# Seven block products instead of eight in the up products of both feed-forward parts of a decoder step

## Chip, cores and metric

The kernel runs on one core of one Trainium2 chip, as one program. The metric is its time on the device in microseconds (us), lower is better.

## What is computed

One inference step of a one-layer decoder on 1024 prompt tokens and 64 sample tokens (1088 columns in all), model width 1024, feed-forward width 2816, in float32. A half feed-forward, a mix of windowed attention and linear attention, and a second half feed-forward follow each other:

```python
def _rmsnorm(x, gain):
    y = xf * lax.rsqrt(jnp.mean(xf * xf, axis=-1, keepdims=True) + EPS)
    return (y * gain.astype(jnp.float32)).astype(x.dtype)

def _half_ffn(x, gain, w1, w3, w2):
    h = _rmsnorm(x, gain)
    return x + 0.5 * ((jax.nn.silu(h @ w1) * (h @ w3)) @ w2)
...
yp = _half_ffn(yp, ffn1_norm, ffn1_w1, ffn1_w3, ffn1_w2)
m, kp, vp, sp = _mix_prompt(_rmsnorm(yp, mix_norm), w_in, ..., w_out)
yp = yp + m
yp = _half_ffn(yp, ffn2_norm, ffn2_w1, ffn2_w3, ffn2_w2)
```

The same three steps run for the sample tokens, whose attention also reads a cache of 2048 rows; the cache windows, shifted by 8 rows, are outputs too.

## The kernel before, in words

Activations stand transposed: `xT` is 128 partitions (a feature within its tile of 128) by 8 tiles by 1088 tokens. Every product of the projections is made of two-part operands. A float32 matrix is split into a high part of type fp32r (by a cast, ScalarE in `split`, L128) and a low part (input minus high part, GpSimd or VectorE, L132), and three matmuls per contraction tile of 128 give high x high, high x low and low x high (`project`, L304 for all products with `hH` and `hL`).

Stages on TensorE, in order: first feed-forward part (0 to about 800 us), projections with linear attention and the sample's attention beside them, prompt attention (to about 1500), output projection (`out_proj`), second feed-forward part (from about 1600 to the end).

A feed-forward part (`ffn`) goes over 22 blocks of 128 features, and for each over three chunks of tokens (`CH`: 364, 362, 362 columns, one PSUM bank each). `project` makes the *up products* h w1 and h w3 of a block (24 matmuls each, PSUM tile `ps1`, shown as `ps`). `gate` multiplies both by 1/rms (`rstd`), applies silu, multiplies them and splits the result into `g`. `h` is x times the gain in two parts, `hH` and `hL`, made tile by tile and chunk by chunk by `norm_part` (L152, L153), which also adds up the squares; `norm_finish` sums these over partitions by a product with ones (L190) and `rsqrt_wide` turns them into 1/rms. After every group of two or three blocks (`GROUPS`) the *down products* (`two`, L255, PSUM tile `ps2`, shown as `ps`) go over 8 output tiles and the three chunks and add into `xT` (L260); w2's blocks `raw2` are split into `hl2` by VectorE alone, in three buffers.

`_Weights` holds the up weights of one block (1 MB, `raw`), loaded two blocks ahead on SP's queue and split one block ahead into `hl` by ScalarE and GpSimd, two instructions of 1024 columns each. `self.copies` are DMA copies of the cache windows in 32 pieces, one issued per block. `out_proj` goes over the eight output tiles and for each over the three chunks (PSUM tile `pso`), and adds into `xT` (L1096); its weights and those of the second part are one sequence in one pool.

Within a pool, the order in which the program is written and a scheduler that works ahead of the run set each engine's instruction order; every engine then works strictly in that order. PSUM has eight banks that rotate (`_Bank`).

## Time and profile before

| | us |
|---|---|
| three runs | 2395.7, 2398.52, 2396.24 |
| median of runs | 2396.24 |
| span of the profiled execution | 2393.6 |
| TensorE busy (matmul) | 2340.4 |
| VectorE busy | 1193.9 |
| ScalarE busy | 675.2 |
| GpSimd busy | 519.4 |

Matmuls are pipelined, so their durations overlap: the time per matmul is read from the distance of their starts, or from a window divided by its count, not from the mean duration. An x behind a group is the number of its instructions, and "idle before" is what its engine waited just ahead of it, with what ended the wait.

### The profile page before, as it was taken

The page shows a single profiled execution, that of the slowest core. Times are in us where ns is not written, and L with a number is a line of the kernel's source. Part 1 is how long each engine was busy: PE and PEld are TensorE (multiplying, and loading weights), DVE is VectorE, ACT ScalarE, POOL GpSimd, SP SyncE. Part 2 cuts the span into 40 slices and gives each one's busy share as a digit, 9 for nine tenths or more (in the row PEclk, how much of TensorE's full clock was granted, in tenths as well). Part 3 has the DMA queues.
Part 4 walks back from the last instruction along what each step waited for, and adds up shares of the span by engine and source line. Part 5 has one row for each costly group of instructions (what it writes and reads, how often), then busy time and mean ns, then how long its engine had stood idle before and what let it go on. Part 6 is the DMA issues. An engine that isn't in the chain of part 4 may idle for free.

```text
span 2393.6 us, 36628 instructions
## 1 busy us (share of the span) xinstructions
PE 2340.4 (98%) x15089; PEld 2201.1 (92%) x15089; DVE 1193.9 (50%) x2434; ACT 675.2 (28%) x1432; POOL 519.4 (22%) x413
## 2 busy tenths in 40 slices
PE   7999999999999998999997999999999999999999
PEld 7999999999999987888775666999999999999999
DVE  8552434344343769655536887445344342434333
ACT  5111020101101523445446777334111101020110
POOL 5011020201100327301104444343101101020100
PEclk9999999999999999999998999999999999999999
DMA  6345542524250341688965432414244333111002
GB/s 196 125 162 189 195 152 97 211 97 154 84 192 28 111 148 55 189 293 310 360 212 152 123 105 86 174 36 162 92 156 157 113 134 141 44 54 45 28 17 85
DMA packets 126023, 327.15 MB, mean 137 GB/s; under 512 B 21040, under 2 KB 96032, under 8 KB 118176
## 3 DMA queue, kind: packets, MB, share of 16 engines
q1 hardware_dynamic: 107232, 313.41, 38.3%
q10 hardware_dynamic: 16512, 5.11, 0.9%
q0 software_dynamic: 2112, 6.29, 0.7%
q8 instruction: 118, 1.93, 0.3%
q14 instruction: 49, 0.40, 0.1%
HBM read 299.49 MB, written 132.64 MB: 181 GB/s over the span
## 4 chain that ended last, share of the span: by engine, by line
PE 89%; DVE 6%; DMA 2%; issue 1%; ACT 1%; POOL 1%; SPq 0%; DVEq 0%; POOLq 0%; ACTq 0%
PE ps L304 43%; PE ps L255 21%; PE psg L304 10%; PE pso L304 4%; PE psO L1030 2%; PE psS L970 2%; PE psT L1009 2%; PE psA L848 1%; PE psW L889 1%; DVE hL L153 1%; PE psD L668 1%; DVE gs L539 1%; PE pss L457 1%; DVE rstd L168 1%; DVE hl L132 1%
## 5 line engine op out<-in xcount | busy, mean ns | idle before, releaser
L304 PE MATMUL ps<-hH,hl 128*128 128x362 f32 (+1 forms) x4224 | 1044.8, 328 | 7.6 <-ACT hl L128 6.8
L304 PEld LDWEIGHTS ps<-hH,hl 128*128 128x128 f32 x4224 | 747.3, 188 | 11.6 <-ACT hl L128 6.8
L304 PE MATMUL ps<-hL,hl 128*128 128x362 f32 (+1 forms) x2112 | 691.9, 328 | 2.2 <-DVE hL L153 1.9
L255 PE MATMUL ps<-g,hl 128*128 128x362 f32 (+1 forms) x3168 | 529.2, 328 | 0.0
L255 PEld LDWEIGHTS ps<-g,hl 128*128 128x128 f32 x3168 | 526.9, 188 | 0.0
L132 POOL TENSOR_TENSOR hl<-raw,hl 128x1024 fp32r<-128x1024 f32 (+1 forms) x98 | 242.8, 2500 | 1212.1 <-ACT hl L128 1211.6
L304 PEld LDWEIGHTS ps<-hL,hl 128*128 128x128 f32 x2112 | 398.0, 188 | 4.2 <-DVE hL L153 2.8
L304 PE MATMUL psg<-hH,hl 128*128 128x384 f32 (+3 forms) x1200 | 311.2, 331 | 0.0
L260 DVE SCALAR_TENSOR_TENSOR xT<-ps,xT 128x362 f32<-128x362 f32 (+1 forms) x384 | 204.3, 534 | 196.9 <-PE ps L255 188.4
L215 ACT ACTIVATE t<-t 128x364 f32<-128x364 f32 x132 | 66.8, 507 | 785.1 <-DVE t L214 784.9
L216 DVE TENSOR_TENSOR t<-ps,rstd 128x364 f32<-128x364 f32 x132 | 70.6, 535 | 417.5 <-PE ps L304 417.5
L304 PEld LDWEIGHTS psg<-hH,hl 128*128 128x128 f32 (+1 forms) x1200 | 209.3, 184 | 10.0 <-issue 5.9
L304 PE MATMUL psg<-hL,hl 128*128 128x384 f32 (+3 forms) x600 | 197.6, 329 | 0.2 <-DVE hL L153 0.2
L128 ACT CAST hl<-raw 128x1024 fp32r<-128x1024 f32 (+2 forms) x148 | 124.3, 885 | 172.4 <-PE ps L304 111.1
L128 ACT CAST g<-t 128x364 fp32r<-128x364 f32 x132 | 65.1, 494 | 346.5 <-DVE t L217 346.4
L132 DVE TENSOR_TENSOR g<-t,g 128x364 fp32r<-128x364 f32 x132 | 107.1, 813 | 93.2 <-ACT g L128 92.8
L214 DVE TENSOR_TENSOR t<-ps,rstd 128x364 f32<-128x364 f32 x132 | 70.5, 535 | 154.4 <-PE ps L304 153.1
L304 PEld LDWEIGHTS psg<-hL,hl 128*128 128x128 f32 (+1 forms) x600 | 110.6, 184 | 6.4 <-issue 3.8
L132 DVE TENSOR_TENSOR hl<-raw,hl 128x384 fp32r<-128x384 f32 (+3 forms) x178 | 107.1, 610 | 7.7 <-ACT hl L128 3.4
L304 PE MATMUL pso<-hH,hl 128*128 128x362 f32 (+1 forms) x384 | 93.7, 325 | 0.2 <-DVE o L1040 0.2
L217 DVE TENSOR_TENSOR t<-t,t 128x364 f32<-128x364 f32 x132 | 74.5, 565 | 17.8 <-ACT t L215 4.1
L990 ACT ACTIVATE e<-e,s 128x128 f32<-128x128 f32 (+3 forms) x96 | 75.4, 786 | 17.3 <-DVE s L977 17.1
(211 smaller groups left out, 2235.8 us busy)
## 6 DMA issues: line engine op xcount, KB each, us to landing
out_wk<-in_ck SPq DMA_DIRECT2D x16, 3060.0 KB
out_wv_s<-in_cv SPq DMA_DIRECT2D x16, 3060.0 KB
kt<-in_kin SPq DMA_DIRECT2D x24, 1280.0 KB
vt<-in_vin SPq DMA_DIRECT2D x60, 512.0 KB
raw<-in_w13b SPq DMA_DIRECT2D x22, 1024.0 KB
raw<-in_w13a SPq DMA_DIRECT2D x21, 1024.0 KB
raw<-in_w2a SPq DMA_DIRECT2D x48, 192.0 KB
raw<-in_w2b SPq DMA_DIRECT2D x48, 192.0 KB
```

The source lines that it names most:

```text
L128: nc.scalar.copy(hi, x)
L132: e.tensor_tensor(out=lo, in0=x, in1=hi.bitcast(F32), op=ALU.subtract)
L214: nc.vector.tensor_tensor(out=t1[:, :n], in0=p1[:, :n], in1=r, op=ALU.mult)
L215: nc.scalar.activation(t1[:, :n], t1[:, :n], AF.Silu)
L216: nc.vector.tensor_tensor(out=t3[:, :n], in0=p3[:, :n], in1=r, op=ALU.mult)
L217: nc.vector.tensor_tensor(out=t3[:, :n], in0=t3[:, :n], in1=t1[:, :n], op=ALU.mult)
L255: self.mm(p[:, :n], lhsT=hl[:, wt, j, :], rhs=g[:, gp, :n], start=i == 0, stop=i == 3 * nf - 1)
L260: nc.vector.scalar_tensor_tensor(out=xs, in0=p[:, :n], scalar=0.5, in1=xs, op0=ALU.mult, op1=ALU.add)
L304: self.mm(p[:m, :n], lhsT=hl[:, wt, k, cs], rhs=h[:, k, h0 : h0 + n], start=i == 0, stop=i == 23)
L970: self.mm(p[:, :mm], lhsT=q[:, 128 * n : 128 * n + 128], rhs=kk[:, o : o + mm], start=x == 0, stop=x == 1,)
L990: nc.scalar.activation(e[:, :w], e[:, :w], AF.Exp, scale=-1.0, bias=s[:, j : j + 1], accum_out=s[:, 2:3])
L1009: nc.tensor.transpose(p[:, j], es[n][:, 128 * k : 128 * k + 128], self.ident)
```

## The change

The up products become block products. A *unit* is now the four blocks A11, A12, A21, A22 of one weight matrix (w1 or w3) for a pair of feature blocks: 128 output features by 512 contraction features each, as one tile of 128 x 4 x 512. The tokens are processed in two halves of 544, and a half's activations are four blocks of 512 features by 272 tokens. `_Factors.prep` makes the seven left operands of a unit (`ORDER`: A11, S1, S2, A12, S3, A22, S4), where the S are sums and differences of the blocks made on GpSimd, and splits each into `op`, of which there are six buffers. `fill` makes the seven right operands for a half of the tokens (`hH[:, 0..6]`, `hL[:, 0..6]`) from x, times gain, times 1/rms, with differences in between. `product` multiplies one left by one right operand (12 matmuls of 272 columns) into one of three PSUM banks X, Y, Z of the unit, some of them on top of one another; `keep` copies a bank out to SBUF and `result` adds such copies to a later state of a bank to get the four outputs of the unit, then applies silu (w1) or multiplies and splits (w3). 1/rms is no longer applied in the gate.

With it: the units are loaded and prepared once for each half; down products go over two chunks of 272 tokens per half, in groups of up to four blocks; `hl2` has two buffers of four blocks and its high part is cast by ScalarE; the output projection goes over four chunks of 272, its last two output tiles half by half; squares are added up by `squares`; the copies of the cache windows are 64 pieces instead of 32; the second part's weight pool is opened behind the output projection. `w13` is laid out for the units on the host.

```diff
-CH = ((0, 364), (364, 362), (726, 362))
+HALF = 544
+Q = 272
+CQ = tuple((Q * c, Q) for c in range(4))
-GROUPS = ((0, 2), (2, 2), (4, 3), (7, 3), (10, 3), (13, 3), (16, 3), (19, 3))
+GROUPS = ((0, 2), (2, 4), (6, 4), (10, 4), (14, 4), (18, 4))
+OPS = 6
...
+class _Factors:
...
+    ORDER = ("A11", "S1", "S2", "A12", "S3", "A22", "S4")
...
+    def prep(self):
+        u, i = divmod(self.made, 7)
+        if u >= len(self.units) // 2 * (self.half + 1):
+            return
+        self.made += 1
+        nc, raw = self.k.nc, self.raw[u]
+        a11, a12, a21, a22 = (raw[:, q] for q in range(4))
+        def add(out, x, y, op):
+            nc.gpsimd.tensor_tensor(out=out, in0=x, in1=y, op=op)
+        if i == 0:
+            src = a11
+        elif i == 1:
+            src = self.pool.tile([P, 512], F32, tag="s1", name="s1", bufs=1)
+            self.s1[u] = src
+            add(src, a21, a22, ALU.add)
+        elif i == 2:
+            add(a21, a11, a21, ALU.subtract)
+            add(a11, self.s1.pop(u), a11, ALU.subtract)
+            src = a11
+        elif i == 3:
+            src = a12
+        elif i == 4:
+            src = a21
+        elif i == 5:
+            src = a22
+        else:
+            add(a12, a12, a11, ALU.subtract)
+            src = a12
+        op = self.pool.tile([P, 2, HALF], F32R, tag="op", name="op", bufs=OPS)[:, :, :512]
+        self.k.split(src, op[:, 0], op[:, 1], el="pool" if i in (3, 5) else "dve")
+        self.op[u, i] = op
+        if i == 6:
+            del self.raw[u]
+            self.load(u + 2)
...
+    def fill(self, pool, H, gain):
         nc = self.nc
+        b = {}
+        def start(j, kh, n):
+            t = pool.tile([P, 4, Q], F32, tag="op", name="fb", bufs=OPS)
+            s = slice(HALF * H + Q * n, HALF * H + Q * n + Q)
+            for k in range(4):
+                nc.scalar.activation(t[:, k], self.xT[:, 4 * kh + k, s], AF.Copy, scale=gain[:, 4 * kh + k : 4 * kh + k + 1])
+            nc.vector.tensor_tensor(
+                out=t, in0=t, in1=self.rstd[:, s].unsqueeze(1).broadcast_to([P, 4, Q]), op=ALU.mult
+            )
+            b[j] = t
+        def put(i, t):
+            hi, lo = self.block(i)
+            nc.scalar.copy(hi, t)
+            nc.vector.tensor_tensor(out=lo, in0=t, in1=hi.bitcast(F32), op=ALU.subtract)
+        def sub(x, y, out):
+            nc.vector.tensor_tensor(out=out, in0=x, in1=y, op=ALU.subtract)
+        start(11, 0, 0)
+        put(0, b[11])
+        start(12, 0, 1)
+        sub(b[12], b[11], b[11])
+        put(1, b[11])
+        start(22, 1, 1)
+        sub(b[22], b[11], b[11])
+        put(2, b[11])
+        start(21, 1, 0)
+        put(3, b[21])
+        sub(b[22], b[12], b[12])
+        put(4, b[12])
+        sub(b[21], b[11], b[21])
+        put(5, b[21])
+        put(6, b[22])
...
+        def product(U, i):
+            n = "XZXYXXZ"[i]
+            first = (U, n) not in banks
+            p = bank(U, n, first)
+            op = w.op.pop((U, i))
+            hi, lo = self.block(i)
+            m = 0
+            for k in range(4):
+                for wt, h in ((0, hi), (0, lo), (1, hi)):
+                    self.mm(
+                        p,
+                        lhsT=op[:, wt, 128 * k : 128 * k + 128],
+                        rhs=h[:, k],
+                        start=first and m == 0,
+                        stop=m == 11,
+                        skip_group_check=True,
+                    )
+                    m += 1
+            w.prep()
+            return p
...
+        def result(U, j, n, p, other=None):
+            u = U % 22
+            f, m = 2 * (u // 2) + j, u % 2
+            if m == 0:
+                t = pool.tile([P, Q], F32, tag="s", name="s", bufs=5)
+                silu[f, n] = t
+                if other is not None:
+                    nc.vector.tensor_tensor(out=t, in0=p, in1=other, op=ALU.add)
+                    p = t
+                nc.scalar.activation(t, p, AF.Silu)
+                return
+            t = pool.tile([P, Q], F32, tag="t", name="t", bufs=4)
+            s = silu.pop((f, n))
+            if other is not None:
+                nc.vector.tensor_tensor(out=t, in0=p, in1=other, op=ALU.add)
+                nc.gpsimd.tensor_tensor(out=t, in0=t, in1=s, op=ALU.mult)
+            else:
+                nc.vector.tensor_tensor(out=t, in0=p, in1=s, op=ALU.mult)
+            if f not in gts:
+                gts[f] = pool.tile([P, 2, HALF], F32R, tag="g", name="g", bufs=5)
+            c = slice(Q * n, Q * n + Q)
+            self.split(t, gts[f][:, 0, c], gts[f][:, 1, c], el="dve")
...
+        def head(U):
+            keep(U, "a", product(U, 0))
+        def body(U):
+            product(U, 1)
+            keep(U, "b", product(U, 2))
+            result(U, 0, 0, product(U, 3), out.pop((U, "a")))
+            keep(U, "c", product(U, 4))
+            result(U, 1, 1, banks[U, "Z"], out.pop((U, "c")))
+        def tail(U):
+            result(U, 1, 0, product(U, 5))
+            result(U, 0, 1, product(U, 6), out.pop((U, "b")))
+            for n in "XYZ":
+                del banks[U, n]
...
-            hl = pool.tile([P, 2, 3, 128], F32R, tag="hl2", name="hl2", bufs=3)
-            self.split(raw[:, :nf], hl[:, 0, :nf], hl[:, 1, :nf], eh="dve", el="dve")
+            hl = pool.tile([P, 2, 4, 128], F32R, tag="hl2", name="hl2", bufs=2)
+            self.split(raw[:, :nf], hl[:, 0, :nf], hl[:, 1, :nf], eh="act", el="dve")
...
+        for H in range(2):
+            late = None
+            head(22 * H)
+            for u in range(22):
+                U = 22 * H + u
+                body(U)
+                if late is not None:
+                    two(H, late)
+                    late = None
+                gi = ends.get(u // 2 * 2 + 1) if u % 2 else None
+                if gi is not None:
+                    for d in range(2):
+                        load2(gi, d)
+                if u < 21:
+                    head(U + 1)
+                tail(U)
+                if gi is not None:
+                    prep2(gi, 0)
+                    late = gi
+                if self.copies and U > 1:
+                    self.tc.keep_in_program_order(self.copies.pop(0)())
+                next(beside, None)
+            if H == 0:
+                self.fill(w.pool, 1, gain)
+                w.half = 1
+                for _ in range(OPS - 1):
+                    w.prep()
             else:
+                before_last()
+            two(H, late)
...
+        order = [(d, c) for d in range(6) for c in range(4)]
+        order += [(d, 2 * H + n) for H in range(2) for d in (6, 7) for n in range(2)]
...
+                        w.load(0, 4)
+                        w.load(1)
+                        for k in (0, 4):
+                            load_x(1, k, 4)
+                        for k in range(8):
+                            for c in range(2):
+                                self.squares(fp, k, c, first=True)
+                        self.norm_finish(fp, ps, (0, 1), False)
+                        w.prep()
+                        self.fill(wp, 0, self.g1)
+                        for _ in range(OPS - 2):
+                            w.prep()
...
+                        self.out_proj(ps, w, row_done)
+                        self.norm_finish(fp, ps, (2, 3), False)
+                    with pool("wts") as wp, pool("ffn") as fp, pool("ps", space=PSUM) as ps0:
+                        ps = _Bank(ps0, 8)
+                        w = _Factors(self, wp, up("w13b"))
+                        w.load(0)
+                        w.load(1)
+                        w.prep()
+                        self.fill(wp, 0, self.g2)
+                        for _ in range(OPS - 2):
+                            w.prep()
...
-        w = np.stack([g[n + "_w1"].reshape(1024, NF, 128), g[n + "_w3"].reshape(1024, NF, 128)], 2)
-        out["w13" + s] = c(w.reshape(8, 128, NF, 256).transpose(2, 1, 0, 3))
+        w = np.stack([g[n + "_w1"], g[n + "_w3"]]).reshape(2, 2, 4, 128, NF // 2, 2, 128)
+        out["w13" + s] = c(w.transpose(4, 0, 3, 5, 1, 2, 6)).reshape(NF, 128, 4, 512)
```

**Places in the order.** A row is a line, an operation, and out<-in by the program's names with a buffer number; x is a repeat.

First place: GpSimd in a stretch of the first part, between two groups of down products. `raw` are a block's or unit's weights, `hl` and `op` the split operands, `s1` the sum S1, `t` a gate's result. Before:

```order
L132 TENSOR_TENSOR hl_964<-raw_552,hl_964 128x1024 x2
L132 TENSOR_TENSOR hl_1162<-raw_969,hl_1162 128x1024 x2
L132 TENSOR_TENSOR hl_1584<-raw_1167,hl_1584 128x1024 x2
L132 TENSOR_TENSOR hl_1778<-raw_1589,hl_1778 128x1024 x2
L132 TENSOR_TENSOR hl_1977<-raw_1783,hl_1977 128x1024 x2
```

Now, somewhat more than one unit's work (L152 additions, L194 low halves, L359 the gate's product):

```order
L152 TENSOR_TENSOR s1_2112<-raw_1936 128x512
L194 TENSOR_TENSOR op_2012<-raw_1783,op_2012 128x512
L152 TENSOR_TENSOR raw_1936<-raw_1936 128x512
L152 TENSOR_TENSOR raw_1783<-raw_1783 128x512
L194 TENSOR_TENSOR op_2046<-raw_1783,op_2046 128x512
L152 TENSOR_TENSOR raw_1936<-s1_2112,raw_1936 128x512
L359 TENSOR_TENSOR t_2117<-t_2117,s_1974 128x272
L152 TENSOR_TENSOR s1_2273<-raw_2079 128x512
L194 TENSOR_TENSOR op_2165<-raw_1936,op_2165 128x512
L152 TENSOR_TENSOR raw_2079<-raw_2079 128x512
```

Where one split of a block stood behind another, additions, low halves and gate products of several units now alternate.

Second place: ScalarE in the same part (L190 is the high half's cast, L339 the copy of a PSUM bank X in `keep`):

```order
L190 CAST hl2_1357<-raw2_1296 128x512
L190 CAST op_931<-raw_609 128x512
L190 CAST hl2_1446<-raw2_1298 128x512
L339 COPY b_934<-psX_833 128x272
L190 CAST op_951<-s1_949 128x512
L190 CAST op_974<-raw_609 128x512
L190 CAST g_957<-t_954 128x272
L190 CAST op_998<-raw_609 128x512
L339 COPY c_977<-psX_833 128x272
L339 COPY a_1001<-psX_985 128x272
L190 CAST op_1015<-raw_609 128x512
L190 CAST op_1034<-raw_609 128x512
```

The casts of `op` stand between copies of `psX`; several operands of a unit are cast ahead of the next copy of that bank, and w2's casts stand among them.

Third place: VectorE at the start of the first part. `hL` is the low half of the activations, `nsq` a square, `nv` and `nt` are steps of 1/rms, `fb` the scaled blocks in `fill`, `qg` and `kg` gains that `constants` loads, `raw2` the first block of w2. Before, in its first rows:

```order
L153 SCALAR_TENSOR_TENSOR hL_78<-xT_85,g1_64,hH_77 128x364
L168 TENSOR_TENSOR rstd_61<-rstd_61,nsq_112 128x364
L153 SCALAR_TENSOR_TENSOR hL_78<-xT_85,g1_64,hH_77 128x364 x2
L168 TENSOR_TENSOR rstd_61<-rstd_61,nsq_120 128x364
L153 SCALAR_TENSOR_TENSOR hL_78<-xT_85,g1_64,hH_77 128x364
L168 TENSOR_TENSOR rstd_61<-rstd_61,nsq_125 128x364
```

Now:

```order
L241 TENSOR_SCALAR nv_162<-psn_160 128x272
L245 SCALAR_TENSOR_TENSOR nt_153<-nt_153,nv_152 128x272
L246 SCALAR_TENSOR_TENSOR rstd_61<-nt_153,rstd_61 128x272
L274 TENSOR_TENSOR fb_173<-fb_173,rstd_61 128x1088
L274 TENSOR_TENSOR fb_199<-fb_199,rstd_61 128x1088
L245 SCALAR_TENSOR_TENSOR nt_163<-nt_163,nv_162 128x272
L1393 TENSOR_SCALAR qg_386<-qg_386 128x1
L1395 TENSOR_SCALAR kg_389<-kg_389 128x1
L282 TENSOR_TENSOR hL_78<-fb_173,hH_77 128x1088
L246 SCALAR_TENSOR_TENSOR rstd_61<-nt_163,rstd_61 128x272
L1404 CAST e2r_402<-e2_400 128x128
L194 TENSOR_TENSOR hl2_577<-raw2_516,hl2_577 128x256
```

The first low half of activations (L282) now stands behind 1/rms, behind the scaling of two blocks and behind `qg` and `kg`; the low half of w2's first block stands ahead of the rest of the fill.

## Rows read from the trace of the kernel before

**Rows 1.** The page: busy time by engine, then the chain that ended last.

```profile
PE 2340.4 (98%) x15089; PEld 2201.1 (92%) x15089; DVE 1193.9 (50%) x2434; ACT 675.2 (28%) x1432; POOL 519.4 (22%) x413
...
PE 89%; DVE 6%; DMA 2%; issue 1%; ACT 1%; POOL 1%; SPq 0%; DVEq 0%; POOLq 0%; ACTq 0%
PE ps L304 43%; PE ps L255 21%; PE psg L304 10%; PE pso L304 4%; PE psO L1030 2%; PE psS L970 2%; PE psT L1009 2%; PE psA L848 1%; PE psW L889 1%; DVE hL L153 1%; PE psD L668 1%; DVE gs L539 1%; PE pss L457 1%; DVE rstd L168 1%; DVE hl L132 1%
```

**Rows 2.** Windows: us, busy us (x instructions) per engine, clock, DMA share, GB/s.

```profile
0.00:25.00 25.00, 12.29 (x39) 10.87 (x40) 19.29 (x24) 14.54 (x29) 16.53 (x19) 0.87 0.80 266
0.00:50.00 50.00, 35.12 (x160) 32.15 (x161) 43.90 (x65) 25.95 (x49) 27.98 (x27) 0.90 0.60 191
300.00:600.00 300.00, 300.00 (x1813) 299.18 (x1813) 115.27 (x210) 43.18 (x70) 45.47 (x18) 1.00 0.39 142
1560.00:2393.00 833.00, 829.96 (x5041) 828.96 (x5039) 340.04 (x623) 140.46 (x234) 133.52 (x64) 1.00 0.26 91
```

**Rows 3.** Instructions by line: matmuls of up and down products.

```profile
L304 PE MATMUL ps<-hH,hl 128*128 128x362 f32 (+1 forms) x4224 | 1044.8, 328 | 7.6 <-ACT hl L128 6.8 <-POOL hl L132 0.8
L304 PE MATMUL ps<-hL,hl 128*128 128x362 f32 (+1 forms) x2112 | 691.9, 328 | 2.2 <-DVE hL L153 1.9 <-DVE kg L1235 0.3
...
L255 PE MATMUL ps<-g,hl 128*128 128x362 f32 (+1 forms) x3168 | 529.2, 328 | 0.0
```

**Rows 4.** Timeline of TensorE, two places: start us, us, engine, line, operation.

```profile
889.18 0.41 PE L553 MATMUL psL<-gh,bor 128*128 128x270 f32 x2
889.43 0.34 PE L304 MATMUL psg<-hL,hl 128*128 128x384 f32 x1
889.61 0.41 PE L553 MATMUL psL<-gh,bor 128*128 128x270 f32 x2
...
1405.42 0.98 PE L1009 MATMUL psT<-ident,e 128*128 128x128 f32 x7
1406.16 0.48 PE L970 MATMUL psS<-kh,q 128*128 128x512 f32 x1
```

**Rows 5.** Instructions by line and shape: xcount, busy us, mean ns, idle before.

```profile
L132 DVE TENSOR_TENSOR hl<-raw,hl 128x512 fp32r<-128x512 f32 x48 | 36.0, 778 | 1.0 <-ACT hl L128 0.6 <-DMA vt<-in_vin 0.2
...
L128 ACT CAST hl<-raw 128x512 fp32r<-128x512 f32 x52 | 29.8, 615 | 44.8 <-PE psg L304 44.8
...
L1012 ACT COPY pt<-psT 128x384 f32<-128x384 f32 x36 | 17.8, 495 | 1.7 <-PE psT L1009 1.5
...
L152 ACT ACTIVATE hH<-xT,g 128x362 fp32r<-128x362 f32 x32 | 17.0, 585 | 1.1 <-DMA xT<-in_xT 0.8 <-PE pso L304 0.4
...
L166 ACT ACTIVATE nsq<-xT 128x362 f32<-128x362 f32 x32 | 15.9, 497 | 6.3 <-POOL rstd L168 6.3
...
L645 DVE TENSOR_TENSOR vx<-psR,cmask 128x1024 f32<-128x1024 f32 x9 | 11.0, 1220 | 0.5 <-ACT kd L640 0.5
```

**Rows 6.** Timeline at 416 us, VectorE, then GpSimd.

```profile
416.19 0.54 DVE L217 TENSOR_TENSOR t<-t,t 128x362 f32<-128x362 f32 x1
418.03 1.50 DVE L132 TENSOR_TENSOR g<-t,g 128x362 fp32r<-128x362 f32 x1 [1.30 <-ACT g L128]
419.55 0.54 DVE L214 TENSOR_TENSOR t<-ps,rstd 128x364 f32<-128x364 f32 x1
...
416.73 5.05 POOL L132 TENSOR_TENSOR hl<-raw,hl 128x1024 fp32r<-128x1024 f32 x2 [54.82 <-ACT hl L128]
```

**Rows 7.** Timeline of the start: GpSimd, then VectorE.

```profile
4.75 0.79 POOL L164 TENSOR_TENSOR nsq<-xT 128x364 f32<-128x364 f32 x1 [3.75 <-DMA xT<-in_xT]
...
13.81 3.11 POOL L132 TENSOR_TENSOR hl<-raw,hl 128x512 fp32r<-128x512 f32 x2
16.88 5.24 POOL L164 TENSOR_TENSOR nsq<-xT 128x362 f32<-128x362 f32 x5
...
17.24 1.12 DVE L153 SCALAR_TENSOR_TENSOR hL<-xT,g,hH 128x364 fp32r<-128x364 f32 x1
18.28 1.12 DVE L168 TENSOR_TENSOR rstd<-rstd,nsq 128x364 f32<-128x364 f32 x1
```

More of the change, by code (lines that the diff above doesn't have):

```diff
@@ L116, in ahead, with __init__, load @@
         self.load(j + 2)
+class _Factors:
+    ORDER = ("A11", "S1", "S2", "A12", "S3", "A22", "S4")
+    def __init__(self, k, pool, units):
+        self.k, self.pool, self.units = k, pool, units
+        self.raw, self.s1, self.op = {}, {}, {}
+        self.made, self.half = 0, 0
+    def load(self, u, parts=2):
+        if u >= len(self.units):
+            return
+        self.raw[u] = self.pool.tile([P, 4, 512], F32, tag="raw", name="raw", bufs=2)
+        n = 4 // parts
+        for q in range(0, 4, n):
+            self.k.nc.sync.dma_start(out=self.raw[u][:, q : q + n], in_=self.units[u][:, q : q + n])
+    def prep(self):
[32 more added lines that the diff above has]
+            self.load(u + 2)
 class _Kernel:
@@ L143, in rsqrt, with squares, scaled @@
         nc.vector.tensor_tensor(out=y, in0=y, in1=t, op=ALU.mult)
-    def norm_part(self, pool, k, c, gain, first=False):
+    def squares(self, pool, k, c, first=False):
         nc = self.nc
-        c0, n = CH[c]
+        c0, n = CQ[c]
         s = slice(c0, c0 + n)
+        x = self.xT[:, k, s]
+        if k == 0:
+            nc.scalar.activation(self.acc[:, s], x, AF.Square)
+            return
+        sq = pool.tile([P, Q], F32, tag="t", name="nsq", bufs=4)
+        if first and k in (2, 5, 7):
+            nc.gpsimd.tensor_tensor(out=sq, in0=x, in1=x, op=ALU.mult)
+        else:
+            nc.scalar.activation(sq, x, AF.Square)
+        e = nc.vector if first else nc.gpsimd
+        e.tensor_tensor(out=self.acc[:, s], in0=self.acc[:, s], in1=sq, op=ALU.add)
+    def scaled(self, k, s, gain):
+        nc = self.nc
         x = self.xT[:, k, s]
@@ new lines, in ffn, with bank, keep @@
+    def ffn(self, pool, ps, w, gain, w2, before_last, after, beside=iter(())):
+        nc = self.nc
+        gts, w2t, raw2 = {}, {}, {}
+        ends = {f0 + nf - 1: gi for gi, (f0, nf) in enumerate(GROUPS)}
+        banks, out, silu = {}, {}, {}
+        def bank(U, n, start):
+            if (U, n) not in banks:
+                banks[U, n] = ps.tile([P, 512], F32, tag="b", name="ps" + n)[:, :Q]
+            return banks[U, n]
+        def product(U, i):
[18 more added lines that the diff above has]
+            return p
+        def keep(U, name, p):
+            t = pool.tile([P, Q], F32, tag="abc", name=name, bufs=6)
+            nc.scalar.copy(t, p)
+            out[U, name] = t
+        def result(U, j, n, p, other=None):
[8 more added lines that the diff above has]
+                nc.scalar.activation(t, p, AF.Silu)
+                return
+            t = pool.tile([P, Q], F32, tag="t", name="t", bufs=4)
[3 more added lines that the diff above has]
+                nc.gpsimd.tensor_tensor(out=t, in0=t, in1=s, op=ALU.mult)
+            else:
+                nc.vector.tensor_tensor(out=t, in0=p, in1=s, op=ALU.mult)
[16 more added lines that the diff above has]
+                del banks[U, n]
@@ L346, in columns @@
             return chunks(j, width, use)
[L348 removed]
+        yield from columns(0, P, G["q"], scale=32.0**-0.5, first=lambda: self.norm_finish(pool, ps, range(4), tag="t1", bufs=2))
         yield from columns(1, P, G["k"])
```

212 lines of the change are left out of this document (70 added, 142 removed).

## The prediction

> **What bounds the kernel now.** I read the busy table and the chain first. TensorE is busy 98% of the span, VectorE 50%, ScalarE 28%, GpSimd 22%, and the chain that ended last lies on TensorE for 89%: 43% in the up products (L304 into ps), 21% in the down products (L255), 4% in the output projection (pso) [rows 1]. Busy time of pipelined matmuls says little about their rate, so I went to the windows and divided time by matmuls. In 300 to 600 us TensorE runs 1813 matmuls in 300 us, 165.5 ns each for 362 or 364 columns; from 1560 us to the end, output projection, hand-over and second part together, it is the same rate, 5041 in 833 [rows 2]. There a matmul saved is time saved, and the hand-over costs nothing today. Only the start is loose: 160 matmuls in the first 50 us, 26.5 us of work, so 23.5 us are lost [rows 2].
>
> The up products are 4224 + 2112 = 6336 matmuls, the down products 3168 [rows 3], the output projection 8 tiles x 3 chunks x 24 = 576: 10,080 in all, 1668 us at 165.5 ns.
>
> **Matmuls, the gain.** Seven products of 12 matmuls per unit, 22 units, two halves, two parts: 7392 up matmuls of 272 columns. Down products go from three chunks of tokens to four: 4224; output projection likewise: 768. Together 12,384. Their spacing: two of 270 columns take 0.25 us (889.18 to 889.43), so 125 ns; 384 columns (889.43 to 889.61) about 180 ns [rows 4]. I take 125 for 272 (123.5 to 127). Seven of 128 columns take 0.74 us, 106 ns [rows 4]: weight loads alone would allow that, so they don't set 125. 12,384 x 0.125 = 1548 us: **-120 us** (-96 to -139). Up products alone give -125, the other two +5.
>
> The Trainium skill ("TensorE: Matmul & The Clock Gate", Back-to-back issue gap) speaks against the change here: in a stream of weight load and matmul pairs it gives about 81 ns per matmul at 128 columns and 131 at 512. By a line through these, an estimate, 10,080 matmuls at 112 ns are 1125 us and 12,384 at 100 ns are 1235: a loss of 110 us. The trace does not agree (165.5 ns at 362, 106 at 128), and the sum goes by the trace.
>
> **Operand preparation, the cost that was covered.** Before, a weight block is split in two GpSimd instructions per feature block and nothing more. Now each unit needs four GpSimd additions of 512 columns and two GpSimd splits, five VectorE splits, seven ScalarE casts, three PSUM copies, and per pair of units three GpSimd multiplications and four VectorE splits of 272. All that has to be made at TensorE's pace, 12 x 0.125 = 1.50 us per product.
>
> ScalarE: 7 x 0.615 + 3 x about 0.4 (0.495 for 384) [rows 5], plus four silu or casts of about 0.4, is 7.1 us of a unit's 10.5. It is covered. GpSimd and VectorE are not independent. At 418.03 a VectorE split of 362 columns takes 1.50 us, where its neighbours of that size take 0.54: two GpSimd splits run from 416.73 on, for 5.05 us [rows 6]. At 16.88 five GpSimd squares take 5.24 us beside alternating VectorE operations that take 1.12, so 1.04 per pair, where one square alone takes 0.79 [rows 7]. So operations that read two SBUF operands take turns, and a VectorE turn of 362 costs GpSimd 0.25 us. VectorE operations with one operand in PSUM keep 0.54 beside GpSimd (419.55) [rows 6] and stay out of it.
>
> Turns per 28 products (four units): a split of 512 on GpSimd is (16.88 - 13.81) / 2 - 0.25 = 1.29 [rows 7]; an unrounded addition of 512 lies between 0.79 x 512 / 364 = 1.11 and 1.29; a multiplication of 272 is 0.59; VectorE's 20 splits of 512 take 0.35 each, its 8 of 272 0.19 (0.25 by columns). Sum: 8 x 1.29 + 16 x (1.11 to 1.29) + 6 x 0.59 + 20 x 0.35 + 8 x 0.19 = 40.1 to 43.0 us, 1.43 to 1.54 us per product if turns follow each other without a gap. Both queues are strictly in order and wait for casts, loads and products; I add 9% to the middle and take 1.62. Were a VectorE operation to hold GpSimd for its whole mean duration (0.78 at 512 [rows 5], so 0.41 at 272), it would be 1.90: bounds 1.43 and 1.90.
>
> What it does to the end: the down products of a group (16 x 1.5 us on TensorE) need few such turns, so six operand buffers fill there. Three of the next 28 products stand among these down products, 25 follow each other. They lose 25 x (1.62 - 1.50) = 3 us of the lead. ScalarE's casts stand four to six products ahead of the PSUM copies that free X (second place of the order, ahead of this), so of the six buffers' lead about 2 us can be lost before a copy stands behind a late cast and TensorE waits. 1 us per stretch, five stretches per half, four halves: **+20 us** (0 at 1.58 or less; 160 at 1.90).
>
> **Four fills.** A fill makes seven sums of activations, scaled by 1/rms, where before products began on each contraction tile as it came. VectorE does 15 operations of 1088 columns, about 1.3 us each (1.22 for 1024 [rows 5]): 19.5 us.
>
> First fill: VectorE's order has qg and kg scaled ahead of the first block's split, and w2's first splits ahead of the second block's (third place of the order, ahead of this). Those loads stand behind both halves of x and two weight units, 6.6 MB; at 266 GB/s [rows 2] that is 25 us. Then 19.5 us of VectorE and about 1.5 of GpSimd turns that no wait hides. In it TensorE does 7 x 1.5 = 10.5 us: lost 25 + 21 - 10.5 = 35.5, and 2 while the lead builds, against 23.5 now: +14.
>
> Fill after the output projection: every block overwrites operands that its last product still reads. After that product come PSUM addition, square, product with ones and the six steps of 1/rms, about 0.5 each (0.497 for a square of 362 [rows 5]), and a GpSimd addition of about 0.8 [rows 7]: 5.4 us; a cast 0.6 and 16 scaled copies of about 0.44 (0.585 for 362), 7 us; a cast of 1088 1.1 and its VectorE half 1.3: TensorE starts some 15.5 us late. Ten VectorE operations (13 us) and five GpSimd turns (6.5) remain, beside which it does 10.5. 24.5 in all, and 2 for the lead: +27.
>
> The two fills between halves stand beside 24 us of down products; VectorE evicts none of these until 12 of its 15 fill operations are issued, eight banks hold 12 us, and the fill begins a few products early: 5 us each, +10. Together **+51** (30 to 80). While TensorE idles its granted clock falls (0.87 on average in 0 to 25 us, between its levels of 1.2 and 2.4 GHz) [rows 2]; a fill paces TensorE anyway.
>
> **Down products.** w2's split buffer goes from three to two, its cast to ScalarE. Between two w2 blocks lie 24 x 0.125 = 3.0 us; cast 0.62, split 0.78, a GpSimd turn ahead 1.29 make 2.7. Nearly covered: **+10** (0 to 60).
>
> DMA: weights are read once per half. By their sizes that is 69 MB more in some 1600 us, 43 GB/s on top of 142 in the first part; 266 was sustained in the first 25 us [rows 2]. A unit loads 1 MB per 10.5 us and a copy now moves half as much at a time. Nothing, unless a load stands behind a copy; that is in the 9%. Projections, attention and the end: unchanged but for one more product with ones.
>
> **Sum.** -120 + 20 + 51 + 10 = -39 on a span of 2393.6 us. The median of runs is 2396.24, 2.6 above the span; on it I get **2357 us**.
>
> **Rivals.** *The shared turns become the bound.* At more than 1.70 us per operand the loss per stretch passes 3 us, the gain is gone, and the kernel is slower. For it: VectorE would be held up at nearly each of 28 splits, as at 418.03; a late GpSimd product holds up a cast, that cast a PSUM copy, that copy TensorE. Against: the packed price is under TensorE's 1.50 or just above. At 1.80: 20 x (25 x 0.30 - 2) = 110 instead of 20, **2447 us**. Chance 0.30. The skill ("SBUF — State Buffer", Who interferes with whom) says the one that starts first holds the shared ports for its whole instruction and the other fully blocks; by that the price nears the 1.90 above. The rows show 0.25 us for a VectorE operation of 0.53, so I stay lower.
>
> *Everything is covered.* At 1.58 or less no stretch waits, w2 keeps up, and fills cost 40: 2396 - 120 + 40 = **2316 us**. For it: gaps that TensorE sees are short, and both engines have much idle time beside the down products. Chance 0.20.
>
> *The smaller matmuls do not stream.* If 272 columns came at 135 ns instead of 125, no gain would be left, because 12,384 x 0.135 is 1668 + 4: some **2480 us** with the losses. Only the short runs of 270 columns say otherwise at that size. Chance 0.04.
>
> **Numbers.** My forecast has 0.46. A measurement of this kernel tells about 0.2% (5 us) from no change. Faster: 0.20 + 0.42 = 0.62; within 5 us: 0.07, from the edges of the forecast and the first rival; slower: 0.31. The range runs from somewhat under the covered case to somewhat over the first rival's 2447: 2300 to 2460, with about one in ten left out at each side.
>
> **What would show it.** Right: 12,384 matmuls at 125 ns inside a stretch; 25 products between down products in about 38.5 us; TensorE waits of 10 to 25 us at the start of each part, on VectorE's hL; VectorE splits of 512 near 1.6 us, GpSimd busy over 80% between down products. Wrong: waits of TensorE on PSUM copies or casts that add up to over 60 us (first rival); no waits outside the fills (second); spacing above 130 ns (third).

## The result and the profile after

The changed kernel takes 2501.5 us (median of 4 runs, 2499.8 to 2505.2) against 2396.0 (4 runs, 2391.9 to 2398.5): a ratio of 1.044, 95% interval 1.043 to 1.046. It is slower by some 105 us where 39 us less were forecast. The profiled execution has a span of 2499.0 us, 105.4 more than before.

The page of the changed kernel, its busy table and its chain, beside [rows 1]:

```profile
PE 2293.5 (92%) x17399; PEld 2131.3 (85%) x17399; DVE 1635.8 (65%) x2780; ACT 1166.9 (47%) x2579; POOL 1206.2 (48%) x1002
...
PE 58%; DVE 13%; POOL 9%; DMA 8%; issue 6%; ACT 4%; SPq 1%; POOLq 0%; DVEq 0%; ACTq 0%
```

TensorE is busy for 47 us less, in a span that is 105 us longer. The chain leaves it for 42% of the span, where it left it for 11%, and GpSimd, which stood at 1%, has 9%.

The windows of the changed kernel, its two parts cut at their fills (beside [rows 2]; length, then busy us and instructions of TensorE, weight loads, VectorE, ScalarE, GpSimd, then the clock). The last row is one piece of the end without a wait:

```profile
0.00:75.60 75.60, 35.25 (x226) 31.81 (x226) 56.41 (x67) 43.08 (x88) 38.91 (x35) 1.00 0.39 127
75.60:432.90 357.30, 330.79 (x2471) 321.01 (x2472) 222.96 (x332) 154.26 (x323) 199.03 (x153) 0.96 0.58 199
432.90:505.00 72.10, 57.57 (x410) 55.39 (x409) 59.18 (x68) 42.36 (x85) 45.08 (x35) 0.86 0.33 110
505.00:874.00 369.00, 352.12 (x2738) 348.30 (x2736) 254.13 (x373) 170.78 (x359) 209.38 (x162) 0.99 0.41 138
1668.10:1725.70 57.60, 36.49 (x228) 33.79 (x228) 44.38 (x49) 36.05 (x71) 35.86 (x23) 0.76 0.13 42
1725.70:2058.40 332.70, 316.44 (x2444) 312.97 (x2443) 221.58 (x319) 142.93 (x305) 190.48 (x142) 0.98 0.53 185
2058.40:2132.10 73.70, 57.82 (x411) 55.57 (x410) 53.53 (x67) 35.18 (x68) 29.94 (x21) 0.86 0.43 138
2132.10:2499.00 366.90, 350.51 (x2737) 346.64 (x2736) 238.56 (x354) 151.93 (x324) 197.74 (x148) 0.99 0.38 123
...
2400.00:2450.00 50.00, 50.00 (x400) 50.00 (x400) 30.13 (x50) 20.08 (x41) 22.94 (x18) 1.00 0.29 85
```

400 matmuls in 50 us are 125 ns each: the price of a matmul of 272 columns was right, and the gain of 120 us is there. What is lost is read as the length of a stretch less 125 ns for each of its up and down matmuls (the rows count a few others too; 75.6 to 432.9 has 2442):

| lost against 125 ns | us | forecast |
|---|---|---|
| start and first fill (0 to 75.6) | 47.9 | 37.5 |
| third fill, after the output projection (1668.1 to 1725.7) | 29.9 | 26.5 |
| two fills between halves (432.9 to 505.0, 2058.4 to 2132.1) | 21.1 + 22.6 | 5 + 5 |
| the rest of the four halves | 52.0 + 27.0 + 27.5 + 25.0 = 131.5 | 30 (20 for stretches, 10 for down products) |
| output projection | 3.4 | 0 |

The sum is 256 us where the forecast's terms make 104. Projections and attention took 694.7 us, before 693.2. So the question is the 131.5, and after it the 43.7.

What one loss in a stretch looks like. The timeline of the changed kernel at 771 us, TensorE:

```profile
771.29 0.29 PE L325 MATMUL psY<-hH,op 128*128 128x272 f32 x1
771.41 0.30 PE L325 MATMUL psX<-hH,op 128*128 128x272 f32 x1
771.54 0.29 PE L325 MATMUL psX<-hL,op 128*128 128x272 f32 x1
773.62 0.52 PE L325 MATMUL psX<-hH,op 128*128 128x272 f32 x2 [1.79 <-DVE op L194]
```

and VectorE, then GpSimd, just ahead of it:

```profile
765.00 0.69 DVE L194 TENSOR_TENSOR op<-raw,op 128x512 fp32r<-128x512 f32 x1 [0.39 <-ACT op L190]
765.61 0.43 DVE L351 TENSOR_TENSOR s<-psZ,c 128x272 f32<-128x272 f32 x1
...
768.61 0.44 DVE L351 TENSOR_TENSOR s<-psZ,b 128x272 f32<-128x272 f32 x1 [0.92 <-PE psZ L325]
770.77 2.79 DVE L194 TENSOR_TENSOR op<-raw,op 128x512 fp32r<-128x512 f32 x2 [1.72 <-ACT op L190]
...
768.80 1.29 POOL L152 TENSOR_TENSOR raw<-raw 128x512 f32<-128x512 f32 x1
770.05 1.29 POOL L194 TENSOR_TENSOR op<-raw,op 128x512 fp32r<-128x512 f32 x1
771.30 1.72 POOL L152 TENSOR_TENSOR raw<-raw 128x512 f32<-128x512 f32 x1
```

The next operand's high half is there, so two matmuls run; the third needs the low half. VectorE makes two of them in 2.79 us beside GpSimd's 1.29 and 1.72, where one alone at 765.00 takes 0.69. Ahead of that VectorE had stood idle, since ScalarE's casts waited for the addition of 768.80. The PSUM additions beside it (765.61, 768.61) keep 0.43. TensorE stands for 1.79 us.

### The profile page after: what moved, and what is told of

Same layout as the page of the kernel before. It is cut to its first block, busy times and chain, and to the rows that moved or that the text cites. A ratio compares the mean times of both kernels' runs of the same rounds, so it can differ in the third digit from the quotient of the medians.

```text
span 2499.0 us, 44684 instructions
## 1 busy us (share of the span) xinstructions
PE 2293.5 (92%) x17399; PEld 2131.3 (85%) x17399; DVE 1635.8 (65%) x2780; ACT 1166.9 (47%) x2579; POOL 1206.2 (48%) x1002
## 4 chain that ended last, share of the span: by engine, by line
PE 58%; DVE 13%; POOL 9%; DMA 8%; issue 6%; ACT 4%; SPq 1%; POOLq 0%; DVEq 0%; ACTq 0%
PE ps L410 19%; PE psg L462 10%; PE psX L325 10%; POOL raw L152 4%; PE psZ L325 4%; PE pso L462 4%; DVE op L194 4%; POOL op L194 2%; ACT op L190 2%; PE psO L1188 2%; PE psY L325 2%; DMA raw<-in_w13b 2%; PE psS L1128 2%; PE psT L1167 2%; DMA raw<-in_w13a 1%
## 5 line engine op out<-in xcount | busy, mean ns | idle before, releaser
L325 PE MATMUL psX<-hH,op 128*128 128x272 f32 x2816 | 606.3, 299 | 68.4 <-DVE op L194 30.1
L410 PE MATMUL ps<-g,hl 128*128 128x272 f32 x4224 | 578.9, 292 | 49.1 <-ACT g L190 17.8
L325 PEld LDWEIGHTS psX<-hH,op 128*128 128x128 f32 x2816 | 477.0, 196 | 83.5 <-DVE op L194 35.9
L194 DVE TENSOR_TENSOR op<-raw,op 128x512 fp32r<-128x512 f32 x352 | 363.2, 1042 | 121.9 <-ACT op L190 119.5
L194 POOL TENSOR_TENSOR op<-raw,op 128x512 fp32r<-128x512 f32 x176 | 257.6, 1463 | 370.3 <-ACT op L190 348.8
L190 ACT CAST op<-raw 128x512 fp32r<-128x512 f32 x528 | 320.1, 621 | 225.0 <-POOL raw L152 144.7
L325 PE MATMUL psX<-hL,op 128*128 128x272 f32 x1408 | 415.7, 295 | 5.3 <-DVE hL L282 5.3
L190 ACT CAST hl<-raw 128x512 fp32r<-128x512 f32 (+3 forms) x250 | 147.4, 602 | 375.3 <-PE ps L410 273.4
L325 PE MATMUL psZ<-hH,op 128*128 128x272 f32 x1408 | 302.7, 291 | 10.9 <-ACT hH L281 10.9
L325 PEld LDWEIGHTS psX<-hL,op 128*128 128x128 f32 x1408 | 276.8, 197 | 6.1 <-DVE hL L282 6.1
L152 POOL TENSOR_TENSOR raw<-raw 128x512 f32<-128x512 f32 x176 | 262.7, 1495 | 3.8
L194 DVE TENSOR_TENSOR hl<-raw,hl 128x512 fp32r<-128x512 f32 (+2 forms) x242 | 188.8, 788 | 53.8 <-ACT hl L190 52.6
L194 DVE TENSOR_TENSOR g<-t,g 128x272 fp32r<-128x272 f32 x176 | 171.4, 977 | 57.5 <-ACT g L190 56.3
L152 POOL TENSOR_TENSOR raw<-s,raw 128x512 f32<-128x512 f32 x88 | 136.2, 1548 | 143.1 <-DVE op L194 142.9
L152 POOL TENSOR_TENSOR s<-raw 128x512 f32<-128x512 f32 x88 | 127.0, 1443 | 108.8 <-DMA raw<-in_w13a 42.1
```

The costliest lines, as they stand in the source:

```text
L152: nc.gpsimd.tensor_tensor(out=out, in0=x, in1=y, op=op)
L190: nc.scalar.copy(hi, x)
L194: e.tensor_tensor(out=lo, in0=x, in1=hi.bitcast(F32), op=ALU.subtract)
L325: self.mm(p, lhsT=op[:, wt, 128 * k : 128 * k + 128], rhs=h[:, k], start=first and m == 0, stop=m == 11, skip_group_check=True,)
L410: self.mm(p, lhsT=hl[:, wt, j, :], rhs=g[:, gp, Q * n : Q * n + Q], start=i == 0, stop=i == 3 * nf - 1,)
```

## The experiments

The runs below were compared on the same sums, since the attention stage takes 7 to 11 us longer in three of them, though nothing was edited there (projections to the output projection: 703.4 without the second fill, 705.5 with five buffers, 701.8 with the pinned fill, 691 to 697 in the others). Lost us by the sums above, from each run's trace:

| run | time | start | rests | fills between | third fill |
|---|---|---|---|---|---|
| changed kernel | 2501.5 | 47.9 | 131.5 | 43.7 | 29.9 |
| no additions | 2393.1 | 45.1 | 40.5 | 33.0 | 27.7 |
| low halves on VectorE | 2468.3 | 46.8 | 95.0 | 44.0 | 30.8 |
| five buffers | 2510.0 | 50.0 | 128.0 | 42.6 | 30.8 |
| no second fill | 2487.5 | 47.5 | 126.6 | 19.3 | 31.3 |
| S2 apart | 2513.4 | 49.2 | 136.4 | 46.0 | 31.8 |
| fill beside down products | 2499.9 | 48.0 | 126.5 | 47.6 | 29.9 |
| three edits | 2470.3 | 48.3 | 95.4 | 44.2 | 31.6 |
| three edits, one low half back | 2476.1 | 49.1 | 103.0 | 46.5 | 31.6 |
| fill pinned | 2494.9 | 48.2 | 129.4 | 31.2 | 29.9 |
| no low halves of VectorE | 2410.6 | 44.9 | 53.1 | 38.8 | 27.3 |
| pinned, low halves on VectorE | 2453.1 | 46.8 | 97.0 | 30.5 | 29.0 |

**No additions.**

```diff
-            add(src, a21, a22, ALU.add)
+            self.s1[u] = src = a21
...
-            add(a21, a11, a21, ALU.subtract)
-            add(a11, self.s1.pop(u), a11, ALU.subtract)
             src = a11
...
-            add(a12, a12, a11, ALU.subtract)
             src = a12
```

> Edit: the four GpSimd additions per unit are left out (S1, S2, S3 and S4 are taken from unmodified blocks), so the output is not the reference's; matmuls, casts, splits, copies and loads stay. In the changed kernel TensorE loses 131 us against 125 ns per matmul in the four halves outside the fills and turnovers. Theory A, the turns of GpSimd and VectorE on two-operand work set the pace of operands: without 16 additions of 1.2 us the turns are 0.8 us per product against TensorE's 1.50, the waits inside the stretches go, and the time is 2380 to 2425 us. Theory B, the order of casts ahead of PSUM copies and the six buffers set it, whatever the additions cost: most of the 131 us stay, over 2460 us.

Measured: 2393.1 us (8 runs), a ratio to the kernel before of 0.999 (0.998 to 1.000), and 40.5 us lost in the rests, 7 of them in the whole second part. Theory A: with GpSimd's additions gone TensorE streams, as a window of this run's last half shows:

```profile
2228.00:2262.00 34.00, 34.00 (x274) 34.00 (x273) 18.54 (x35) 11.22 (x22) 4.03 (x4) 1.00 0.27 86
```

Every load of the changed kernel is still made here, and in its twelve stretches of at least 195 up matmuls after 300 us TensorE loses 0.7 us in all: the 8% of the chain that lie on DMA are not what slows the stretches. The run also shows the other half of the answer: even with all additions free this kernel is no faster than before, since its start and fills lose 106 us and the rests 40.

**GpSimd's low halves to VectorE.**

```diff
-        self.k.split(src, op[:, 0], op[:, 1], el="pool" if i in (3, 5) else "dve")
+        self.k.split(src, op[:, 0], op[:, 1], el="dve")
```

> Edit: the two low halves per unit that GpSimd makes (A12, A22) go to VectorE; nothing else changes. Theory A: a low half costs the shared turns about 0.35 us on VectorE where it costs 1.29 on GpSimd, so the turns fall from 1.5 to about 1.2 us per product and most waits in the stretches go: 2400 to 2450 us. Theory C, VectorE's own queue becomes the bound: seven low halves of 1.04 us, two of gates of 0.98 and about 2.5 us of PSUM work per unit are 11.7 us where TensorE needs 10.5: 2510 us or more.

Measured: 2468.3 us (4 runs), between the two theories: 33 us of 105 came back, the rests fell from 131.5 to 95.0. A low half on VectorE is cheaper for the shared turns than one on GpSimd, by much less than the 0.94 us (1.29 less 0.35) that I had. From the traces: in the stretches of at least 195 up matmuls after 300 us (the one beside the third fill left out), the time in which GpSimd or VectorE is in an operation without a PSUM operand is 1.49 us per product in the changed kernel (0.877 of 1.70) and 1.40 here (0.857 of 1.63). Per 28 products that is 2.5 us for eight low halves, 0.3 each. VectorE is busier in these stretches (79% where it was 66%) and TensorE still faster, so VectorE's own queue alone was not the limit.

**Five operand buffers.**

```diff
-OPS = 6
+OPS = 5
```

> Edit: five operand buffers instead of six. Theory A, pace: a stretch starts with one operand less in store and loses up to 1.5 us more, 20 stretches: 2505 to 2530 us. Theory B, lead: each stop at a late cast or copy is cut into by one product's time, several stops per stretch: over 2540 us.

Measured: 2510.0 us (2 runs), which looks like theory A, but the 9 us are the attention stage's. In the feed-forward parts nothing changed (251.4 lost against 253.0). Neither theory: taking the sixth buffer away costs nothing, so it holds no lead that a stretch could live on.

**S2 in a tile of its own.**

```diff
-            add(a11, self.s1.pop(u), a11, ALU.subtract)
-            src = a11
+            src = self.pool.tile([P, 512], F32, tag="s2", name="s2", bufs=1)
+            add(src, self.s1.pop(u), a11, ALU.subtract)
+            self.s2 = src
...
-            add(a12, a12, a11, ALU.subtract)
+            add(a12, a12, self.s2, ALU.subtract)
...
-            t = pool.tile([P, Q], F32, tag="abc", name=name, bufs=6)
+            t = pool.tile([P, Q], F32, tag="abc", name=name, bufs=5)
```

> Edit: S2 gets a tile of its own instead of overwriting A11 (paid for with one copy buffer less, five instead of six), so its addition no longer waits for VectorE's low half of A11, for which GpSimd waited 142.9 us in all in the changed kernel (88 additions). Theory A1, the chain: additions come late because each waits in order behind VectorE, and the wait goes: 2440 to 2475 us. Theory A2, the turns alone: as many operations share the same turns, 2490 to 2510 us.

Measured: 2513.4 us (2 runs). The wait is gone and the time isn't:

```profile
L152 POOL TENSOR_TENSOR s<-s,raw 128x512 f32<-128x512 f32 x88 | 142.2, 1615 | 1.5
```

against, in the changed kernel,

```profile
L152 POOL TENSOR_TENSOR raw<-s,raw 128x512 f32<-128x512 f32 x88 | 136.2, 1548 | 143.1 <-DVE op L194 142.9
```

A1 falls, and the time is just over A2's range. GpSimd's idle time only moved: it waits 365 us for VectorE ahead of the gate's product (78 in the changed kernel) and 113 us for loads ahead of S1 (73). So this wait in order was slack, not the limit; the additions run beside more of VectorE's work and take longer (1.62 for 1.55).

**No low halves of VectorE.**

```diff
-        self.k.split(src, op[:, 0], op[:, 1], el="pool" if i in (3, 5) else "dve")
...
+        if i in (3, 5):
+            self.k.split(src, op[:, 0], op[:, 1])
...
+        else:
+            nc.scalar.copy(op[:, 0], src)
...
-                        lhsT=op[:, wt, 128 * k : 128 * k + 128],
+                        lhsT=op[:, wt * low, 128 * k : 128 * k + 128],
```

> Edit: the five low halves per unit that VectorE makes are left out (their matmuls take the high half in its place, so the output is not the reference's); GpSimd keeps its four additions and two low halves. Theory A, turns that both engines share: GpSimd's additions fall from 1.49 to under 1.37 us, the turns from 1.49 to about 1.1 us per product, and the halves outside fills and turnovers lose 60 us or less instead of 131: 2395 to 2430 us. Theory D, GpSimd's own queue (74% busy in a stretch) sets it and VectorE only waits: two thirds of the 131 stay, over 2460 us.

Measured: 2410.6 us (2 runs); rests 53.1. Theory A again, from the other side: GpSimd keeps all its work (69% busy in the stretches, 70% in the changed kernel), loses only its neighbour, and TensorE streams; so GpSimd's own queue alone is not the limit either. This run's additions, by line and shape:

```profile
L152 POOL TENSOR_TENSOR raw<-raw 128x512 f32<-128x512 f32 x176 | 241.8, 1381 | 3.6
L152 POOL TENSOR_TENSOR raw<-s,raw 128x512 f32<-128x512 f32 x88 | 117.6, 1336 | 130.1 <-ACT op L178 129.7
```

In the changed kernel the first of these took 1.495 us. The edit also takes one step out of the way from an addition to TensorE; the run with S2 apart says that one such step in order does not count, but turns and steps were not told apart by a run of their own.

**No second fill.**

```diff
-                self.fill(w.pool, 1, gain)
```

> Edit: the fill between the two halves of each part is left out, so the second half multiplies the first half's activations and the output is not the reference's. TensorE loses 21.1 and 22.6 us in the two turnovers. If VectorE's fill ahead of the gates' low halves causes it, a turnover then loses about 5 us as any other group does, and the time is about 2465 us (2455 to 2475). If the last gates would come too late for the down products anyway, less than 15 us are won: over 2485 us.

Measured: 2487.5 us (2 runs), 9.4 and 9.9 us lost at the two places instead of 21.1 and 22.6; 9 of these 24 us were given back in the attention stage. So about half of the loss there is the fill's; what the other half is, no run shows.

**Fill beside the down products, then pinned.** The first run issued the fill in eight pieces between the output tiles:

```diff
-                self.fill(w.pool, 1, gain)
...
-            two(H, late)
+                two(H, late, self.fill(w.pool, 1, gain))
...
+                next(meanwhile, None)
```

> Edit: the fill for the second half is issued in eight pieces between the output tiles of the last group's down products instead of ahead of them. In the changed kernel the two turnovers lose 21.1 and 22.6 us, without the fill 9.4 and 9.9. If the place in VectorE's order is what costs: 10 to 13 each, about 2478 us (2468 to 2488). If VectorE has not the room beside 24 us of down products (15 fill operations of about 1.4 us, 16 evictions of 0.44, 8 low halves of 0.8 are 34 us): no gain, over 2490 us.

Measured: 2499.9 us (2 runs), nothing. It was no test: the scheduler put the fill into VectorE's order as early as ever. The second run pins its four scalings:

```diff
+            if H:
+                self.tc.keep_in_program_order(i)
```

> Edit: as the run with the fill beside the down products, whose VectorE order turned out to be the old one, but with the four scalings of that fill pinned behind the evictions traced ahead of them, so that in VectorE's order the gates' low halves and the first evictions now stand ahead of the fill. If that place is what costs, the two turnovers lose 8 to 13 us each instead of 21.1 and 22.6: 2468 to 2486 us. If VectorE has not the room beside the down products: over 2490 us.

Measured: 2494.9 us (2 runs). The losses became 19.9 and 11.3, but the fourth half's rest rose from 25.0 to 34.6 and the second's fell from 27.0 to 22.5: over all the feed-forward parts 14 us came back, where 28 did with the fill left out, and 7 of the 14 went to a slower attention stage. The first place won nothing to speak of (21.1 to 19.9) and the second almost as much as leaving the fill out (22.6 to 11.3, where that run has 9.9). The time lies in the range of the second expectation; corrected for the attention stage it lies between the two. How much of the loss is the place in the order and how much VectorE's length is not shown.

**Combinations.** All three edits (low halves, S2, unpinned fill), then with one low half back on GpSimd:

> Edit: three together: both of GpSimd's low halves on VectorE, S2 in a tile of its own, the fill beside the down products. With the low halves moved GpSimd waited 563 us for VectorE ahead of the S2 additions. Theory A1, that chain holds the operands back: the halves outside fills and turnovers lose 40 us or less (95 with the low halves moved alone), 2385 to 2415 us. Theory A2 or a VectorE that is full: 2430 to 2460 us.

> Edit: as the run with three edits, but one low half per unit (A22) stays on GpSimd. If VectorE's length is the limit there, this is 10 us or more faster than that run; if the shared turns are, 10 us or more slower; within 10 us neither decides.

Measured: 2470.3 and 2476.1 us (4 runs each), the second 6 us slower, which decides nothing by itself. Only the low halves count, as in their own run. And the pinned fill with the low halves:

> Edit: the pinned fill and both of GpSimd's low halves on VectorE. If the two gains are separate, 33 us for the low halves and what the pinned fill alone brings: 2440 to 2455 us. If VectorE, which now has two more low halves per unit, is full at the turnovers: 2460 us or more.

Measured: 2453.1 us (4 runs), ratio 1.024 (1.022 to 1.026): the two gains add up, and this is the fastest version that leaves nothing out. It does not beat the kernel before.

## Why the prediction was wrong

**Matmuls: right.** 12,384 at 125 ns, as the window from 2400 us shows. The Trainium skill's two figures ("TensorE: Matmul & The Clock Gate", Back-to-back issue gap: about 81 ns at 128 columns, 131 at 512) give some 100 ns at 272, an estimate by a line through them. The trace does not agree at this width either: 125 ns.

**Turns: the size was right, what they do to TensorE was not.** Forecast were 1.43 to 1.54 us of shared turns per product and 9% of gaps, 1.62 us per product. Measured: 1.49 us of turns, 12% of gaps, 1.70 us (587 us for 346 products in the stretches after 300 us, TensorE's waits and clock included). The step that failed is the next one: "of the six buffers' lead about 2 us can be lost", so that a stretch costs 1 us. Nothing of the kind was taken off: 21 products of a stretch (not 25), 0.20 us late each, are 4 us, and the 17 stretches lost 68 us, 4.0 each. The run with five buffers loses no more, so the sixth held no lead. With 20 stretches that alone is 80 instead of 20. The mechanism in the text was that of the first rival, and its point, 1.70 us per operand, is what was measured; but the rival's sum still took those 2 us off.

Nor did TensorE stop where that step said, at a PSUM copy behind a late cast. Its waits ahead of up products, those for activations (hH, hL) left out (us in all, times, longest):

```profile
PE psX L325 <- DVE op L194: 30.1, 19, 2.6
...
PE psX L325 <- ACT op L190: 15.4, 17, 2.8
...
PE psY L325 <- POOL op L194: 7.6, 4, 4.5
...
PE psX L325 <- ACT b L339: 5.0, 3, 2.5
...
PE psX L325 <- ACT c L339: 2.6, 2, 2.1
```

It waits for the operands themselves, 53.1 us, the low halves most of all, and 7.6 us for copies. Of the signs named for the forecast, VectorE's splits near 1.6 us and GpSimd over 80% busy did not come either (1.04 us on average, 70% in the stretches).

Set side by side, the runs show what the turns are worth. Per product in the stretches, turns and TensorE's time are 1.49 and 1.70 us in the changed kernel, 1.40 and 1.63 with the low halves on VectorE, 1.15 and 1.51 without VectorE's low halves, 1.04 and 1.50 without the additions. Why 12 to 14% of the time stays without a turn in the first two was not traced further than the wait at 771 us, where VectorE stood idle for a cast that waited for GpSimd.

**A wait costs TensorE's clock too.** For the stretches this was not in the sum at all. Windows of the changed kernel around a wait of 1.78 us that ends at 365.7:

```profile
362.00:366.00 4.00, 2.22 (x18) 2.00 (x17) 3.17 (x3) 2.26 (x5) 3.31 (x4) 1.00 0.26 59
366.00:369.40 3.40, 3.40 (x17) 3.40 (x16) 1.63 (x4) 1.56 (x3) 2.72 (x3) 0.50 0.65 241
369.40:372.00 2.60, 2.60 (x22) 2.60 (x22) 1.91 (x3) 1.44 (x4) 2.60 (x3) 0.99 0.00 0
```

The granted clock falls to 0.50, the level of 1.2 GHz: 17 matmuls in 3.4 us, where full speed does 27, so 1.3 us more. The clock's records show 14 such pieces of 3.4 us in the four rests (and one of 10.2 about the wait for w2), some 18 of the 131.5 us; ten of them lie in the 17 stretches, 13 of their 68 us. At the two places between halves it is a piece of 20.5 us each, in each about 26 matmuls at the lower level's spacing: under 3 us of the 21 and 23 lost there. Not every wait brings one: after that of 771 us the clock stayed at 1.00.

**The turns' price, as the Trainium skill puts it.** By the rule of the Trainium skill ("SBUF — State Buffer", Who interferes with whom) the one that starts first holds the shared ports for its whole instruction and the other waits. The trace agrees. In the rows at 771 us GpSimd's low half, begun first, keeps its 1.29 us and ends at 771.34. VectorE's first low half, begun during it, ends at 771.89, 0.55 later. The addition that GpSimd began at 771.30 ends 1.13 after that, and VectorE's second low half 0.55 after the addition. It is so in the whole changed kernel: 265 low halves of 512 columns that VectorE began during a GpSimd operation end 0.55 us (median) after the latter, 0.546 to 0.553 in the middle eight tenths; 287 GpSimd operations of 512 columns that began during a two-operand operation of VectorE end 1.15 us (median) after it; 178 that VectorE joined later keep 1.29.

So an operation that has waited needs a little less after its turn begins than one that starts free (0.55 for 0.69, 1.15 for 1.29), and a pair in turn costs 1.70 us where the forecast's 0.35 and 1.29 make 1.64: nearly right. The reason given for staying below the rule was not: the rows at 16.88 fit it too (VectorE ends 0.40 us after GpSimd, GpSimd 0.64 after VectorE, 1.04 per pair), and the 1.90 came from a mean of 0.78 that has waits in it. By these figures a low half moved to VectorE saves 0.60 us, not 0.94; eight would be 4.8 of the 7.5 us that I had, and 2.5 were measured. What became of the rest was not traced.

**Fills.** The first and the third were forecast at 37.5 and 26.5 and lost 47.9 and 29.9. VectorE's fill operations took 1.4 to 1.6 us on average beside GpSimd instead of 1.3, and the first matmuls of the first ran slower (last section). The two between halves were the large miss: "5 us each". That step looked only at evictions in VectorE's order. Its order also has the fill ahead of the last gates' low halves, for which the down products wait. The waits of TensorE from 434 to 506 us:

```profile
PE ps L410 <- ACT g L190: 7.9, 3, 4.1
PE ps L410 <- DVE g L194: 5.7, 2, 3.1
```

and two rows of VectorE there, with TensorE's wait for the second:

```profile
449.45 3.04 DVE L282 TENSOR_TENSOR hL<-fb,hH 128x1088 fp32r<-128x1088 f32 x2
...
454.22 1.50 DVE L194 TENSOR_TENSOR g<-t,g 128x272 fp32r<-128x272 f32 x1
...
455.77 1.27 PE L410 MATMUL ps<-g,hl 128*128 128x272 f32 x4 [3.10 <-DVE g L194]
```

**Down products.** No 10 us for w2's buffers as such, but the first half lost 25 us more than the others. One wait of it is 9.0 us for the cast of a w2 block at 244 us, for whose load ScalarE had waited 7.2 us. The loads and stores of the attention's biases stand on the same queue there, but nothing was run to tell whether they held it up, and the rest of these 25 us was not traced to single causes.

By these numbers the sum is 2357 + 101 for the rests + 34 and 14 for the fills + 3, 2509, against 2501.5 measured. The 8 us over are about what the kernel before lost elsewhere than at its start (2393.6 less 1668, 23.5 and 693.2), which the forecast carried along.

## What to carry to other kernels

A sum of work that two engines must do in turns, set against the pace of the engine that they feed, is a rate that wants room: here 1.49 and 1.40 us against TensorE's 1.50 were too close, with queues in strict order, and 1.15 was not. What each item is late was lost times the number of items, and a few buffers of lead took nothing off here. Multiplying fewer blocks is worth what the makers of the operands have to spare, not what TensorE saves: with 65% and 48% busy, VectorE and GpSimd seemed to have room, and together they had none. When a step is put into a queue, look for every consumer behind it there, not only for the one that the step concerns.

## What the runs showed of the hardware that was not expected

TensorE's first matmuls ran at half speed, and the clock's row says nothing of it. In the changed kernel from 28 to 45 us:

```profile
28.00:45.00 17.00, 6.21 (x24) 5.59 (x25) 13.81 (x16) 6.79 (x10) 0.82 (x1) 1.00 0.19 48
...
42.64 0.66 PE L325 MATMUL psZ<-hH,op 128*128 128x272 f32 x2
43.09 0.43 PE L325 MATMUL psZ<-hL,op 128*128 128x272 f32 x1
43.32 0.66 PE L325 MATMUL psZ<-hH,op 128*128 128x272 f32 x2
```

Three matmuls in 0.68 us are 227 ns each, the spacing that the pieces at 0.50 have too (three from 366.23 to 366.91). The row's 1.00 is no measurement: the clock's records in this trace begin at 45.2 us, with one at full speed, and a window without a record shows 1.00. From 46 us on the matmuls came every 125 ns. In the kernel before the records begin at 15.1 us: ahead of that its matmuls of 364 columns came every 0.30 us, from 15.3 to 16 us every 0.17, so the 0.87 of [rows 2] is too high for the same reason. At the start of a trace the spacing between matmuls is the surer sign of the speed.

The other thing is how exactly VectorE and GpSimd wait for each other, to some hundredths of a microsecond, where the forecast took a mean price.
